# A decoder trunk's first stage: weights in halves of the contraction, half of the tokens later, tables on ScalarE's queue

## The chip, the core and the metric

The kernel runs on one NeuronCore of a Trainium2 chip. It is one launch. The metric is the device time of that launch in microseconds (us). Five engines work side by side, each with its own in-order queue: TensorE (PE, matrix products and transposes; PEld is its load of the stationary operand), VectorE (DVE), ScalarE (ACT), GpSimd (POOL) and SyncE (SP). Transfers from memory are asked for on SP's or ACT's queue ("SPq", "ACTq" in the profile) and run on 16 DMA engines.

## What is computed

Two decoder layers over 512 tokens of 1024 channels, in float32. The part that the change touches is the very beginning, the first even mixer's input projection:

```python
def even_mixer(x, w_in, conv_w, pool_w, pool_scale, w_out):
    p = x @ w_in                                   # 512 x 1024 by 1024 x 2048
    y_a = short_gated_conv(p[..., :3 * D_A], conv_w)
    y_b = multiscale_pool(p[..., 3 * D_A:], pool_w, pool_scale)
    return jnp.concatenate([y_a, y_b], axis=-1) @ w_out

for layer in range(DEPTH):                         # DEPTH = 2: even_mixer, then odd_mixer
    x = layer_norm(ALPHA * x + mix, ...)
    x = layer_norm(ALPHA * x + swiglu(x, ...), ...)
```

`odd_mixer` (forgetting attention beside a 31-tap convolution) and the two `swiglu` blocks follow. The parameter tables of both mixers' convolutions (`ev_conv_w`, `ev_pool_scale`, `od_dw_w`, `od_dw_b`, `od_cn_g`, `od_cn_b`) and the 4 x 128 x 128 matrix `ev_pool_w` are small inputs beside the weights.

## The kernel before

**Numbers.** Each float32 operand is split into a rounded part and a rest (`split`, L84 to L87: ACT copies the rounded part, `hi`; DVE or POOL subtracts it from the source, `lo`). A product is three matmuls that add into one PSUM bank: hi x hi, hi x lo, lo x hi (`mm3`, L89 to L92). So every weight costs one transfer, one ACT copy and one DVE or POOL subtraction before PE can use it.

**Tokens.** The 512 tokens are four tiles of 128 (`x0` to `x3`, 512 KB each). PE transposes each tile in eight 128 x 128 blocks (`transpose_x`, L128 to L150), and `split` makes `xh` and `xl` of them, channels on partitions. All later products stream `xh` and `xl`.

**The first block.** The last 512 columns of `w_in` feed the pooling mixer in four groups of 128 columns. Groups 0 and 1 come first: `START = "x0 x1 w0G x2 x3 w1G"` asks on SP's queue for two token tiles, the first weight block (all 1024 rows of 128 columns, `w0`), the other token tiles and the second weight block (`w1`). "G" says that POOL makes the `lo` part. `project(pus, ws, HALF)` then forms group 0 and group 1 for tokens 0 to 255 and for tokens 256 to 511: 2 x 2 x 8 x 3 = 96 matmuls with 256 columns, into two PSUM banks, `pus`. Six matmuls of the identity with itself (`WARM`, L125) run ahead of the first transpose.

**Tables.** `params()` asks on ACT's queue for six row tables (38 rows of 512 in all, `rows`), transposes them on PE (L575) and copies them to `par`. `pool_params()` loads `ev_pool_w` on SP's queue and splits it. `ln_params()` loads six rows of 8 x 128 on SP's queue and transposes them (L190).

**Order.** The framework's scheduler sets the order on all engines of this stage from a timeline that it estimates; inside `tc.manual_schedule` blocks the engines named there keep the order in which the code is written. Later stages (both SwiGLU blocks, PE in the attention) are in such blocks already. Each engine, and each of the two issuing queues, takes its instructions strictly in order. A transfer reports on one of eight counters, `DMAHW0` to `DMAHW7`, which are given out in turn; a transfer that is given a counter whose last transfer has not landed waits, at its place in the issuing engine's queue, until it has.

Of the kernel before, what the change touches and what calls it, by code (L numbers as in the profile page):

```python
# [10 lines left out]
F32 = mybir.dt.float32  # L11
F32R = mybir.dt.float32r
# [5 lines left out]
P = 128  # L18
# [6 lines left out]
DH = 512  # L25
# [10 lines left out]

CP = 900
WARM = 6
START = "x0 x1 w0G x2 x3 w1G"
SPLIT = [(0, 256), (256, 512)]  # L40
FIRST = 2
PLAIN = 4
# [18 lines left out]
def trunk(ctx, tc, x, ev_w_in, ev_conv_w, ev_pool_w, ev_pool_scale, ev_w_out, od_w_in,  # L61
          od_forget_b, od_dw_w, od_dw_b, od_cn_g, od_cn_b, od_w_out,
          ln_mix_g, ln_mix_b, ln_ffn_g, ln_ffn_b, ffn_w_in, ffn_w_out, out):
    nc = tc.nc
# [3 lines left out]
    rawp = pool("raw", 3)  # L68
    wtp = pool("wt", 8)
# [9 lines left out]
    def tpsum():  # L79
        return psum("tp")  # L80
# [3 lines left out]
    def split(hi, lo, src, eng=None):  # L84

        nc.scalar.activation(hi, src, AF.Copy)  # L86
        (eng or nc.vector).tensor_tensor(lo, src, f32(hi), op=ALU.subtract)  # L87
# [17 lines left out]
    def load_cols(w, c0, **kw):  # L105
        return load_split(w[:, c0:c0 + P].rearrange("(k p) c -> p k c", p=P), [KD, P], **kw)
# [8 lines left out]
    xs = [res.tile([P, D], F32, tag=f"x{t}", name=f"x{t}") for t in range(NT)]  # L115
    xh = res.tile([P, KD, S], F32R, tag="xh", name="xh")
    xl = res.tile([P, KD, S], F32R, tag="xl", name="xl")
# [10 lines left out]
    def transpose_x(t, gbt=None, tags=("tp", "tp")):  # L128

        for half in range(2):  # L130
            tp = psum(tags[half])
            for j in range(4):
                k = half * 4 + j
                nc.tensor.transpose(tp[:, j * P:(j + 1) * P], xs[t][:, k * P:(k + 1) * P], ident)
            src = tp
            if gbt is not None:
                src = wk.tile([P, S], F32, tag="sg", name="xt")
                for j in range(4):
                    k = half * 4 + j
                    blk = slice(j * P, (j + 1) * P)  # L140
                    if j < XA:
                        nc.scalar.activation(src[:, blk], tp[:, blk], AF.Identity,
                                             scale=gbt[:, 0, k:k + 1], bias=gbt[:, 1, k:k + 1])
                    else:
                        nc.vector.tensor_scalar(src[:, blk], tp[:, blk], gbt[:, 0, k:k + 1], gbt[:, 1, k:k + 1],
                                                op0=ALU.mult, op1=ALU.add)
            dst = (slice(None), slice(half * 4, half * 4 + 4), slice(t * P, (t + 1) * P))
            split(xh[dst], xl[dst], src.rearrange("p (j q) -> p j q", q=P))

    def project(accs, ws, ranges):  # L150

        for a, b in ranges:
            for acc, (wh, wl) in zip(accs, ws):
                for k in range(KD):
                    mm3(acc[:, a:b], wh[:, k, :], wl[:, k, :], xh[:, k, a:b], xl[:, k, a:b],
                        k == 0, k == KD - 1)

    ALL = [(0, S)]
# [405 lines left out]
    def params():  # L564

        rows = wk.tile([38, DH], F32, tag="sg", name="rows")
        nc.scalar.dma_start(rows[0:3, :], ev_conv_w[0])
        nc.scalar.dma_start(rows[3:4, :], ev_pool_scale)
        nc.scalar.dma_start(rows[4:35, :], od_dw_w[0])
        nc.scalar.dma_start(rows[35:36, :], od_dw_b)  # L570
        nc.scalar.dma_start(rows[36:37, :], od_cn_g)
        nc.scalar.dma_start(rows[37:38, :], od_cn_b)
        tp = tpsum()
        for j in range(4):
            nc.tensor.transpose(tp[:, j * 38:(j + 1) * 38], rows[:, j * P:(j + 1) * P], ident[:38, :38])  # L575
        nc.vector.tensor_copy(par, tp[:, :152].rearrange("p (j r) -> p j r", r=38))

    def even_mixer():
        w_in = ev_w_in[0]
# [4 lines left out]
        with tc.tile_pool(name="even", bufs=1) as ep:  # L584
# [3 lines left out]

            def pool_params():
                pwr = rawp.tile([P, 4, P], F32, tag="raw", name="pwr")  # L590
                nc.sync.dma_start(pwr, ev_pool_w[0].rearrange("g c d -> c g d"))
                pwh = ep.tile([P, 4, P], F32R, tag="pwh", name="pwh")
                pwl = ep.tile([P, 4, P], F32R, tag="pwl", name="pwl")
                split(pwh, pwl, pwr)
                return pwh, pwl
# [28 lines left out]
                                               op0=ALU.mult, op1=ALU.subtract)  # L624

            ws = []
            for item in START.split():
                i = int(item[1])
                if item[0] == "x":
                    nc.sync.dma_start(xs[i], x[0, i * P:(i + 1) * P, :])  # L630
                    transpose_x(i, tags=(("tp", "tp"), ("sc", "sc"), ("py", "cv"), ("tp", "tp"))[i])
                else:
                    ws.append(load_cols(w_in, 3 * DH + i * P, eng=nc.gpsimd if item[2] == "G" else None))
            pus = [psum("fl"), psum("fl")]
            project(pus, ws, HALF)
            pw = pool_params()
            params()
            ln_params()
            z = [pool_in(pus[g], g) for g in range(2)]
            for g in range(2, 4):  # L640
                w = load_cols(w_in, 3 * DH + g * P)
                pu = psum()
                project([pu], [w], ALL)
                z.append(pool_in(pu, g))
                pool_out(g - 2, *z[g - 2])
            for j in range(4):
# [454 lines left out]
```

## Time and profile before

| | |
|---|---|
| device time, 3 runs | median 1083.24 us (1083.21 to 1085.02) |
| the profiled execution, its own time | 1084.19 us |
| its span, first to last instruction | 1082.5 us |
| mean granted TensorE clock | 0.987 of full speed |
| PE busy | 1046.3 us, 97% |
| DVE, ACT, POOL busy | 744.3, 482.6, 179.5 us |
| DMA | 108.49 MB, mean 100 GB/s |

In timelines a row gives the start in us from the span's start, the duration, the engine, the line, the operation, out<-in and the count; in brackets stand the engine's idle time before the row and what ended it. In the tables by windows each engine has its busy time and, in brackets, its instructions; then come the granted clock of PE, the share of the 16 DMA engines that was busy, and the GB/s moved. A matmul's row is longer than its share of PE's time, since matmuls overlap: the step from one start to the next is what one costs in a row of many.

### The profile page before, as it was taken

Reading aid. Unit: us, or ns where it says so; the run is one execution under the profiler, and the core shown is the slowest. Engines: PE = TensorE matmul, PEld = TensorE weight load, DVE = VectorE, ACT = ScalarE, POOL = GpSimd, SP = SyncE. Lnnn points to the kernel's source line nnn. Section 1 sums busy time; section 2 is a strip of 40 time slices with the busy share of each in tenths; the row PEclk is TensorE's granted clock in tenths of the full one; section 3 lists DMA queues with packets and bytes.
Section 4 is the critical chain, followed back from the end, with each engine's and each line's share of the span. In section 5 each row is a group of like instructions: output and inputs, shape, how many; then the busy total and the mean of one; then the engine's idle time right before and its main releaser. Section 6 shows DMA issues by size and latency. Waiting matters only on the chain.

```text
span 1082.5 us, 16331 instructions
## 1 busy us (share of the span) xinstructions
PE 1046.3 (97%) x6631; PEld 938.1 (87%) x6631; DVE 744.3 (69%) x1027; ACT 482.6 (45%) x711; POOL 179.5 (17%) x163
## 2 busy tenths in 40 slices
PE   7999999999799999999999899999999799999997
PEld 7888889899688999988979777889899688999986
DVE  3845466888562788756479988466888562788746
ACT  4432233545321455443466889533545321455520
POOL 2000300000000000012499983610000000000003
PEclk8999999999899999999999999999999899999999
DMA  6433501631332431360233332311531333440522
GB/s 205 120 98 104 168 1 45 189 99 41 116 117 92 143 121 37 120 191 21 58 101 98 95 104 59 118 39 43 190 99 41 117 115 101 134 130 28 163 71 78
DMA packets 113482, 108.49 MB, mean 100 GB/s; under 512 B 5257, under 2 KB 94905, under 8 KB 113407
## 3 DMA queue, kind: packets, MB, share of 16 engines
q1 hardware_dynamic: 112784, 107.11, 32.2%
q8 instruction: 52, 0.85, 0.3%
q10 hardware_dynamic: 622, 0.34, 0.1%
q14 instruction: 24, 0.19, 0.1%
HBM read 103.17 MB, written 2.10 MB: 97 GB/s over the span
## 4 chain that ended last, share of the span: by engine, by line
PE 81%; DVE 8%; ACT 4%; issue 3%; DMA 2%; POOL 1%; SPq 0%; POOLq 0%; ACTq 0%; DVEq 0%
PE fl L388 14%; PE fl L91 9%; PE fl L92 9%; PE fl L90 9%; PE sc L388 7%; PE sc L91 5%; PE sc L92 5%; PE sc L90 5%; DVE sw L380 3%; PE py L91 2%; PE py L90 2%; PE py L92 2%; DVE sum L369 2%; PE cv L388 2%; PE cv L92 2%
## 5 line engine op out<-in xcount | busy, mean ns | idle before, releaser
L86 ACT ACTIVATE w<-raw 128x1024 fp32r<-128x1024 f32 x104 | 109.0, 1057 | 207.8 <-PE sc L91 77.9
L388 PE MATMUL fl<-T,sw 128*128 128x256 f32 x1296 | 160.5, 279 | 4.3 <-DVE sw L380 1.5
L388 PEld LDWEIGHTS fl<-T,sw 128*128 128x128 f32 x1296 | 153.9, 188 | 6.9 <-ACT u L396 2.5
L87 DVE TENSOR_TENSOR w<-raw,w 128x1024 fp32r<-128x1024 f32 x76 | 92.4, 1223 | 92.1 <-ACT w L86 91.7
L87 POOL TENSOR_TENSOR w<-raw,w 128x1024 fp32r<-128x1024 f32 x28 | 67.3, 2413 | 424.3 <-ACT w L86 410.7
L376 ACT ACTIVATE sw<-sum 128x1024 fp32r<-128x1024 f32 x72 | 76.0, 1060 | 104.6 <-DVE sum L369 73.5
L380 DVE TENSOR_TENSOR sw<-sum,sw 128x1024 fp32r<-128x1024 f32 x72 | 88.0, 1222 | 26.2 <-ACT sw L376 26.2
L388 PE MATMUL sc<-xh,sw 128*128 128x256 f32 x576 | 105.5, 278 | 0.0
L388 PEld LDWEIGHTS sc<-xh,sw 128*128 128x128 f32 x576 | 89.9, 188 | 0.1
L380 DVE TENSOR_TENSOR sw<-q,sw 128x1024 fp32r<-128x1024 f32 x54 | 65.4, 1221 | 29.2 <-ACT sw L376 29.1
L168 POOL TENSOR_TENSOR rs<-rs,neghalf 128x1 f32<-128x1 f32 x20 | 13.6, 681 | 402.2 <-DVE rs L167 396.2
L388 PE MATMUL sc<-xl,sw 128*128 128x256 f32 x288 | 80.1, 278 | 0.0
L90 PE MATMUL fl<-w,hh 128*128 128x512 f32 (+1 forms) x176 | 69.7, 396 | 8.8 <-ACT w L86 8.8
L376 ACT ACTIVATE sw<-q 128x1024 fp32r<-128x1024 f32 x54 | 56.3, 1050 | 45.3 <-DMA q<-in_ffn_w_in 45.3
L91 PE MATMUL fl<-w,hh 128*128 128x512 f32 (+1 forms) x176 | 69.6, 395 | 1.6 <-DVE w L87 1.6
L92 PE MATMUL fl<-w,hl 128*128 128x512 f32 (+1 forms) x176 | 69.3, 394 | 0.0
L704 DVE SCALAR_TENSOR_TENSOR cv<-hp,par,cv 128x512 f32<-128x512 f32 x84 | 63.1, 751 | 5.8 <-ACT cv L692 4.5
L369 DVE TENSOR_TENSOR sum<-q,q 128x1024 f32<-128x1024 f32 x36 | 43.9, 1219 | 25.7 <-DMA q<-in_ffn_w_in 25.7
L388 PE MATMUL fl<-xh,sw 128*128 128x256 f32 x288 | 53.8, 281 | 1.6 <-DVE sw L380 1.6
L91 PE MATMUL sc<-xl,w 128*128 128x256 f32 (+1 forms) x168 | 55.0, 329 | 0.0
L90 PE MATMUL sc<-xh,w 128*128 128x256 f32 (+1 forms) x168 | 54.9, 331 | 0.0
L92 PE MATMUL sc<-xh,w 128*128 128x256 f32 (+1 forms) x168 | 54.8, 328 | 0.0
(413 smaller groups left out, 2666.1 us busy)
## 6 DMA issues: line engine op xcount, KB each, us to landing
q<-in_ffn_w_in SPq DMA_DIRECT2D x72, 512.0 KB
raw<-in_ffn_w_out SPq DMA_DIRECT2D x44, 512.0 KB
raw<-in_od_w_in SPq DMA_DIRECT2D x20, 512.0 KB
raw<-in_ev_w_in SPq DMA_DIRECT2D x16, 512.0 KB
raw<-in_ffn_w_in SPq DMA_DIRECT2D x16, 512.0 KB
raw<-in_ev_w_out SPq DMA_DIRECT2D x8, 512.0 KB
raw<-in_od_w_out SPq DMA_DIRECT2D x8, 512.0 KB
x<-in_x SPq DMA_DIRECT2D x4, 512.0 KB
```

The source lines that it names most:

```text
L86: nc.scalar.activation(hi, src, AF.Copy)
L87: (eng or nc.vector).tensor_tensor(lo, src, f32(hi), op=ALU.subtract)
L90: nc.tensor.matmul(acc, lh, rh, start=start, stop=False)
L91: nc.tensor.matmul(acc, lh, rl, start=False, stop=False)
L92: nc.tensor.matmul(acc, ll, rh, start=False, stop=stop)
L168: nc.gpsimd.tensor_tensor(rs[:, 1:2], rs[:, 0:1], neghalf, op=ALU.pow)
L369: nc.vector.tensor_tensor(raw[name], raw[a], raw[b], op=ALU.add)
L376: nc.scalar.activation(g["A"][name][0], g["raw"][self.LEFT[name]], AF.Copy)
L380: nc.vector.tensor_tensor(lo, g["raw"][self.LEFT[name]], f32(hi), op=ALU.subtract)
L388: nc.tensor.matmul(acc, l[:, k, cols], r[:, k, :], start=start and i == k == m == 0, stop=stop and i == 1 and k == 3 and m == 2, skip_grou ...
L704: V.scalar_tensor_tensor(acc if i == KCONV - 1 else part, hp[:, i:i + S], tap(i), part, op0=ALU.mult, op1=ALU.add)
```

## The change

In the first block only:

- **First weights in halves of k.** Instead of two blocks of 1024 rows by 128 columns, two of 512 rows by 256 columns are loaded: `w0` holds rows 0 to 511 for groups 0 and 1, `w1` rows 512 to 1023. The same bytes are loaded, and the same 96 matmuls run, in four parts of 24: `A0` (first half of k, tokens 0 to 255), `A1` (second half of k), `B0`, `B1` (tokens 256 to 511). Within a part all hi x hi products come first, then hi x lo, then lo x hi.
- **Queues.** SP's queue asks for `x0`, `x1`, `w0`; ACT's queue asks, behind its first copies, for `w1` ("d1"), `x2`, `x3` ("d2", "d3"), the six tables ("pp") and, later, `ev_pool_w`.
- **Fill.** Twelve further matmuls of the identity with itself ("ww") stand behind the transposes of `x1`.
- **Order by hand.** PE, ACT and DVE keep the written order through the first block, `ev_pool_w`'s split and the split of the weights of groups 2 and 3. The tables' transposes come behind it. `w0`'s lo part moves from POOL to DVE; `w1`'s stays on POOL.

```diff
-START = "x0 x1 w0G x2 x3 w1G"
+KEEP = 12
+FIRSTS = "x0 d1 x1 d2 d3 pp w0 ww A0 w1 x2 A1 x3 B0 B1"
...
             def pool_params():
                 pwr = rawp.tile([P, 4, P], F32, tag="raw", name="pwr")
-                nc.sync.dma_start(pwr, ev_pool_w[0].rearrange("g c d -> c g d"))
+                nc.scalar.dma_start(pwr, ev_pool_w[0].rearrange("g c d -> c g d"))
...
-            for item in START.split():
-                i = int(item[1])
-                if item[0] == "x":
-                    nc.sync.dma_start(xs[i], x[0, i * P:(i + 1) * P, :])
-                    transpose_x(i, tags=(("tp", "tp"), ("sc", "sc"), ("py", "cv"), ("tp", "tp"))[i])
-                else:
-                    ws.append(load_cols(w_in, 3 * DH + i * P, eng=nc.gpsimd if item[2] == "G" else None))
             pus = [psum("fl"), psum("fl")]
-            project(pus, ws, HALF)
-            pw = pool_params()
-            params()
+            def first_block(i, a, b):
+                wh, wl = ws[i]
+                for m, (w, xt) in enumerate(((wh, xh), (wh, xl), (wl, xh))):
+                    for g, acc in enumerate(pus):
+                        for k in range(4):
+                            nc.tensor.matmul(acc[:, a:b], w[:, k, g * P:(g + 1) * P], xt[:, 4 * i + k, a:b],
+                                             start=i == m == k == 0, stop=i == 1 and m == 2 and k == 3)
+            raws = [rawp.tile([P, 4, 2 * P], F32, tag="raw", name="raw") for _ in range(2)]
...
+            load_x(0, nc.sync)
+            load_x(1, nc.sync)
+            load_w(0, nc.sync)
+            later = {1: lambda: load_w(1, nc.scalar), 2: lambda: load_x(2, nc.scalar),
+                     3: lambda: load_x(3, nc.scalar)}
+            with tc.manual_schedule(engines={mybir.EngineType.PE, mybir.EngineType.Activation,
+                                             mybir.EngineType.DVE}):
+                for item in FIRSTS.split():
+                    if item == "ww":
+                        for _ in range(KEEP):
+                            nc.tensor.matmul(warmup[:, :P], ident, ident, start=True, stop=True)
+                        continue
+                    if item == "pp":
+                        params_transposed = params()
+                        continue
+                    i = int(item[1])
+                    if item[0] == "x":
+                        transpose_x(i, tags=(("tp", "tp"), ("sc", "sc"), ("py", "cv"), ("tp", "tp"))[i])
+                    elif item[0] == "d":
+                        later[i]()
+                    elif item[0] == "w":
+                        ws.append([wtp.tile([P, 4, 2 * P], F32R, tag="wt", name="w") for _ in range(2)])
+                        split(*ws[i], raws[i], nc.gpsimd if i else None)
+                    else:
+                        first_block(i, *HALF["AB".index(item[0])])
+                pw = pool_params()
+                wn = [load_cols(w_in, 3 * DH + g * P) for g in (2, 3)]
+            params_transposed()
```

ACT's queue at the start of the program, before the change. `xh_78` are copies of transposed tokens out of PSUM, `w_145` the hi part of `w0` out of `raw_143`, `rows_289` the six tables; the waits are on counters of engines and transfers.

```order
L567 DMA rows_289<-in_ev_conv_w 3x512
L123 ACT_TABLE_LOAD
L123 ACTIVATE warm_85<-warm_85 128x1 [waits DVE_49]
L568 DMA rows_289<-in_ev_pool_scale 1x512
L569 DMA rows_289<-in_od_dw_w 31x512
L570 DMA rows_289<-in_od_dw_b 1x512
L571 DMA rows_289<-in_od_cn_g 1x512 [waits DMAHW1_49]
L86 ACTIVATE xh_78<-tp_114 128x4x128 [waits PE_49]
L572 DMA rows_289<-in_od_cn_b 1x512 [waits DMAHW3_49]
L86 ACTIVATE xh_78<-tp_121 128x4x128 [waits PE_49]
L86 ACTIVATE xh_78<-sc_129 128x4x128 [waits PE_49]
L86 ACTIVATE w_145<-raw_143 128x1024 [waits DMAHW4_49]
```

All six tables are asked for ahead of the second token copy, and `w0`'s copy comes behind three token copies. The same queue now, from the copies of `x1` (`sc`) to the copies of the two weight halves (`raw_115` is `w0`, `raw_116` is `w1`):

```order
L87 ACTIVATE xh_78<-sc_137 128x4x128 [waits PE_49]
L87 ACTIVATE xh_78<-sc_144 128x4x128 [waits PE_49]
L646 DMA x2_76<-in_x 128x1024
L646 DMA x3_77<-in_x 128x1024
L575 DMA rows_153<-in_ev_conv_w 3x512
L576 DMA rows_153<-in_ev_pool_scale 1x512 [waits DMAHW1_49]
L577 DMA rows_153<-in_od_dw_w 31x512 [waits DMAHW3_49]
L578 DMA rows_153<-in_od_dw_b 1x512 [waits DMAHW5_49]
L579 DMA rows_153<-in_od_cn_g 1x512 [waits DMAHW7_49]
L580 DMA rows_153<-in_od_cn_b 1x512 [waits DMAHW1_49]
L87 ACTIVATE w_160<-raw_115 128x1024 [waits DMAHW2_49]
L87 ACTIVATE w_200<-raw_116 128x1024
```

The tables now stand between the token copies and the weight copies. In this program the counters go to the transfers in this order: `x0` 0, `x1` 1, `w0` 2, `w1` 3, `x2` 4, `x3` 5, `ev_conv_w` 6, the first row of `ln_params` 7; `ev_pool_scale` gets 1 again, `od_dw_w` 3, `od_dw_b` 5, `od_cn_g` 7 and `od_cn_b` 1 for a third time.

PE's queue before, from the identity matmuls (L126) over the token transposes (L134) to the first products (L90 to L92):

```order
L126 MATMUL cv<-ident 128x128 x6
L134 MATMUL tp<-ident,x_74 128x128 x8
L134 MATMUL sc<-ident,x_75 128x128 x8
L134 MATMUL py<-ident,x_76 128x128 x4
L134 MATMUL cv<-ident,x_76 128x128 x4
L90 MATMUL fl<-xh,w 128x256
L91 MATMUL fl<-xl,w 128x256
L134 MATMUL tp<-ident,x_77 128x128 x8
L92 MATMUL fl<-xh,w 128x256
```

And now (L664 are the twelve fill matmuls, L640 the products; `x_74` to `x_77` are the token tiles):

```order
L135 MATMUL sc<-ident,x_75 128x128 x8
L664 MATMUL cv<-ident 128x128 x12
L640 MATMUL fl<-xh,w 128x256 x8
L640 MATMUL fl<-xl,w 128x256 x8
L640 MATMUL fl<-xh,w 128x256 x8
L135 MATMUL py<-ident,x_76 128x128 x4
L135 MATMUL cv<-ident,x_76 128x128 x4
L640 MATMUL fl<-xh,w 128x256 x8
L640 MATMUL fl<-xl,w 128x256 x8
L640 MATMUL fl<-xh,w 128x256 x8
L135 MATMUL tp<-ident,x_77 128x128 x8
```

The transposes of `x2`, which PE took as soon as `x1` was done, now stand behind part `A0`, and those of `x3` behind `A1`. In the odd layer's attention the estimated timeline has also swapped some neighbours on ACT, DVE and POOL; PE's order there is the same.

More of the change, by code (lines that the diff above doesn't have):

```diff
@@ L566, in params, with transposed @@
         rows = wk.tile([38, DH], F32, tag="sg", name="rows")
+        def transposed():
+            tp = tpsum()
+            for j in range(4):
+                nc.tensor.transpose(tp[:, j * 38:(j + 1) * 38], rows[:, j * P:(j + 1) * P], ident[:38, :38])
+            nc.vector.tensor_copy(par, tp[:, :152].rearrange("p (j r) -> p j r", r=38))
         nc.scalar.dma_start(rows[0:3, :], ev_conv_w[0])
@@ L572, in params @@
         nc.scalar.dma_start(rows[37:38, :], od_cn_b)
[L573 to L576, printed above, removed]
+        return transposed
     def even_mixer():
@@ new lines, in even_mixer, with load_x, load_w @@
+            raws = [rawp.tile([P, 4, 2 * P], F32, tag="raw", name="raw") for _ in range(2)]
+            def load_x(i, eng):
+                eng.dma_start(xs[i], x[0, i * P:(i + 1) * P, :])
+            def load_w(i, eng):
+                eng.dma_start(raws[i], w_in[i * DH:(i + 1) * DH, 3 * DH:3 * DH + 2 * P].rearrange(
+                    "(k p) c -> p k c", p=P))
+            load_x(0, nc.sync)
[3 more added lines that the diff above has]
+                     3: lambda: load_x(3, nc.scalar)}
@@ L640, in even_mixer @@
             for g in range(2, 4):
-                w = load_cols(w_in, 3 * DH + g * P)
                 pu = psum()
-                project([pu], [w], ALL)
+                project([pu], [wn[g - 2]], ALL)
                 z.append(pool_in(pu, g))
```

## The prediction, on record before the result

> **What bounds the kernel now.** I read three views in this order: PE's waits, the first microseconds on PE and ACT in order of time, and the same stretch by windows. From the start to 210 us PE waits for others like this:
>
> ```profile
> PE py L134 <- DMA x<-in_x: 4.6, 1, 4.6
> PE cv L126 <- POOL sum L606: 1.6, 1, 1.6
> PE fl L388 <- DVE sw L380: 1.0, 2, 0.8
> PE fl L388 <- ACT sw L376: 0.7, 1, 0.7
> PE tp L134 <- DMA x<-in_x: 0.2, 1, 0.2
> ```
>
> Between the wait for a token tile (`py` holds the transposes of `x2`) and the first Strassen products (L388, in the SwiGLU) PE has none. So whatever PE gains or loses in the first block it keeps one for one: the stages behind it are tied to PE's progress, and no transfer there is asked for at a fixed time. The question is when PE finishes the 96 products of the first block. The stretch on PE and ACT:
>
> ```profile
> 1.56 2.93 PE L126 MATMUL cv<-ident 128*128 128x128 f32 x12 [1.56 <-POOL sum L606]
> 4.67 1.63 PE L134 MATMUL tp<-ident,x 128*128 128x128 f32 x8 [0.18 <-DMA x<-in_x]
> 6.14 1.04 PE L134 MATMUL sc<-ident,x 128*128 128x128 f32 x8
> 6.34 0.60 ACT L86 ACTIVATE xh<-tp 128x512 fp32r<-128x512 f32 x1
> 10.40 1.06 ACT L86 ACTIVATE w<-raw 128x1024 fp32r<-128x1024 f32 x1 [2.97 <-DMA raw<-in_ev_w_in]
> 11.54 2.36 POOL L87 TENSOR_TENSOR w<-raw,w 128x1024 fp32r<-128x1024 f32 x1 [9.81 <-ACT w L86]
> 11.82 1.11 PE L134 MATMUL py<-ident,x 128*128 128x128 f32 x4 [4.64 <-DMA x<-in_x]
> 13.44 0.56 PE L90 MATMUL fl<-xh,w 128*128 128x256 f32 x1
> 26.91 0.28 PE L91 MATMUL fl<-xl,w 128*128 128x256 f32 x1
> 27.03 0.28 PE L92 MATMUL fl<-xh,w 128*128 128x256 f32 x1
> 27.24 0.44 PE L575 MATMUL tp<-ident,rows 38*128 38x38 f32 x4
> 27.68 0.50 PE L90 MATMUL fl<-xh,w 128*128 128x512 f32 x1
> ```
>
> PE stops at 7.18, goes on at 11.82 with `x2`, and from there runs without a gap to 27.24, where the tables' transposes follow the last product: 15.42 us for 16 transposes and 96 products. A product in the row costs the step between starts, 0.12 us. Part of the 15.42 is spent at half clock:
>
> ```profile
> 5.82:9.24 3.42, 1.36 (x12) 1.12 (x10) 1.88 (x3) 1.60 (x3) 0.00 (x0) 1.00 1.07 355
> 9.24:12.65 3.41, 0.83 (x4) 0.83 (x5) 0.67 (x1) 1.54 (x2) 1.11 (x1) 0.50 0.95 278
> 12.65:16.06 3.41, 3.41 (x18) 3.41 (x17) 1.72 (x4) 1.89 (x4) 1.25 (x1) 0.50 0.09 23
> 16.06:19.48 3.42, 3.42 (x31) 3.42 (x30) 2.49 (x3) 2.25 (x4) 1.90 (x1) 1.00 0.54 153
> ```
>
> The columns are PE, PEld, DVE, ACT, POOL, then clock, DMA share and GB/s. The clock falls to 0.50 at 9.24, while PE is idle, and comes back at 16.06. PE works 4.24 us at half speed and loses 2.12 us by it.
>
> **What the change takes away.** The first weights come late because of the tables. At 13 to 16 us DMA is 9% busy, and still SP waits for `x3` and `w1` (it can issue behind them only at 13.16 and 14.82):
>
> ```profile
> 1.71 0.30 ACTq L569 DMA_DIRECT2D rows<-in_od_dw_w  x1
> 2.04 0.34 ACTq L570 DMA_DIRECT2D rows<-in_od_dw_b  x1
> 4.65 0.23 ACTq L571 DMA_DIRECT2D rows<-in_od_cn_g  x1
> 5.98 0.38 SPq L97 DMA_DIRECT2D raw<-in_ev_w_in  x1
> 13.16 0.27 SPq L188 DMA_DIRECT2D rows<-in_ln_ffn_b  x1
> 14.82 0.27 SPq L188 DMA_DIRECT2D rows<-in_ln_mix_b  x1
> rows<-in_od_dw_w ACTq DMA_DIRECT2D x1, 62.0 KB
> ```
>
> About one engine in sixteen is late with its share, and a table of 62 KB was asked for just ahead of `w0`. The Trainium skill, "DMA: Bandwidth & Descriptors", section "Why a DMA increments its semaphore by 16 and not by 1", says that a transfer is spread over the largest number of engines up to 16 that divides its slowest dimension; 31 rows would all go to one engine, which agrees with this tail. With the tables behind `x3`, `w0` should land where the rate puts it: `x1` has landed at 5.98 (SP's next issue waited for it), plus 512 KB at 355 GB/s, 1.48 us, gives 7.4 instead of 10.4. That is the change's possible gain.
>
> **What it adds.** The queue order of ACT has the tables between the copies of `x1` and the copy of `w0`, and three of their issues wait at that place for a transfer to land: `od_dw_w` for `w1`, `od_dw_b` for `x3`, `od_cn_b` for `ev_pool_scale`. That such a wait holds ACT is in the rows above: `od_cn_g` was free to go at 2.38 and went at 4.65, when `x0` had landed and PE began its transposes at 4.67. So `w0`'s copy, `w1`'s copy and the copies of `x2` and `x3` all stand behind the landing of `x3`, and every product of part `A0` behind `w0`'s copy. PE's transposes of `x2`, which filled the wait before, stand behind `A0`.
>
> When does `x3` land? ACT can ask for `w1` with the second copy of `x0`, at about 6.4, and for `x2` and `x3` with the second copy of `x1`, whose transposes end at 7.18: about 7.3 and 7.7 (two issues took 0.86 us on SP):
>
> ```profile
> 0.80 0.86 SPq L630 DMA_DIRECT2D x<-in_x  x2
> 185.81 3.60 DMA q<-in_ffn_w_in
> ```
>
> The second row, from the chain of waits, is a block of 512 KB with nothing ahead of it: 3.60 us from issue to landing. So `w1` lands at 10.0, `x2` and `x3` 1.48 us behind each other, `x3` at 12.9. Bounds: alone it would land at 7.7 + 3.6 = 11.3; at most as late as before, about 13.1. I take 12.9, since the rate of 355 GB/s is held over the whole stretch before. The Trainium skill, the same page, section "Issuing engines are not separate DMA queues", says that a second issuing queue saves issue time only; by it too the three blocks share one rate and the sum stands.
>
> Then three more issues (0.34 + 0.23 + 0.23), so `w0`'s copy starts at 13.7 and ends at 14.76; with 0.09 of passing on, as from 11.46 to POOL's start at 11.54 before, PE starts `A0` at 14.85.
>
> **The sum.**
> - PE resumes at 14.85 instead of 11.82: +3.03 us.
> - The work from there is the same, 16 transposes and 96 products. PE has been idle from the end of the fill to 14.85. The fill costs twelve times what a warm-up matmul costs at full clock: six took 2.93 at half, so twelve take 2.93, and they end at 10.1. That is 4.74 us of idle against 4.64 before, so the half-clock loss is the same: 0. The fill is hidden by the wait. If the wait were gone, it would hold `A0` until 10.1.
> - `lo` of `w0` (now on DVE) and of `w1` (POOL, 2.36 us behind a copy that ends at about 15.8) are ready before their products: the first to need one stands 16 products of twice 0.12 behind 14.85, at 18.7. 0.
> - `B0` follows `x3`'s transposes at once and needs the first copy (0.60) of them, of which half is covered by the second four transposes: +0.25.
> - Behind the block, after the tables' transposes (0.44, from 27.24 to 27.68) come the products of groups 2 and 3. They need their weight copies, which stand on ACT behind `ev_pool_w`. That is asked for at about 24.7, with the second copy of `x3`; 256 KB take between 2.9 (3.60 less half of 1.48) and 3.6 us. The copies of it and of two weights, about 0.6 + 2 x 1.06, then end between 30.3 and 31.0, against a need at 30.5 + 0.44 = 30.95: 0, with a cover of 0.7 at most.
> - Fewer rows on SP, DVE instead of POOL for `w0`: beside PE's work, 0.
>
> In all +3.3 us. Against the profiled execution's own 1084.19 (span 1082.5) that is 1087.5; this execution is 0.95 above the median of the runs shown, 1083.24, so on the median's footing the forecast is **1086.5 us**, 0.3% slower.
>
> **Rivals.**
>
> *A: `x3` lands early and the clock holds.* At the bound 11.3, `w0`'s copy ends at 13.16 and PE starts at 13.25, 3.15 us behind the fill. If the clock stays up, the end moves by 13.25 - 11.82 - 2.12 + 0.25 = -0.4 us; if it drops for one window of 3.41 us, by +1.3: about 1084, no change. By the Trainium skill, "TensorE: Matmul & The Clock Gate", Part 1, the clock is judged over free-running windows of some 3.4 us and drops after an idle one, so that a gap of 4.74 would often not contain a whole idle window, and then even the forecast's start would cost only +1.2 us, 1084.4. The trace has the windows (9.24 and 16.06 are two of them apart), but not that mildness:
>
> ```profile
> 596.32:599.74 3.42, 1.02 (x4) 0.86 (x5) 3.25 (x6) 3.28 (x8) 3.42 (x4) 1.00 0.02 5
> 599.74:603.15 3.41, 3.41 (x13) 2.58 (x12) 3.37 (x8) 2.16 (x5) 3.33 (x4) 0.50 0.43 108
> ```
>
> Here a window with PE 30% busy was enough for the drop. A gap of 4.74 us takes at least 2.37 us out of some window, a third busy at most. So A needs the early landing.
>
> *B: the copies are not held (faster).* If ACT reached `w0` at its landing, 7.4, and behind the token copies at 8.0, `w0` would be copied by 9.1, PE would go from the fill at 10.1 straight into `A0` at full clock, and the block would last 15.42 - 2.12 + 0.25 = 13.55 us, to 23.7: -3.6 us, 1079.6. It decides itself by whether ACT's copy starts before about 9. For it speaks the early landing of `w0`; against it the waits in ACT's order.
>
> *C: the held-back work comes due (slower still).* `ev_pool_w` late by the 3.6 bound and copies of the sums out of the two banks behind it (both groups now end together, where group 0's bank was free at 25.77) leave DVE with `pwl`, two weights' `lo` and both groups' window sums at once. DVE was busy 16.4 of 20 us between 40 and 60, so a backlog of 3 to 4 us is absorbed late, and PE could stand 1 to 3 us more: 1088.5.
>
> ```profile
> 20.00:40.00 20.00, 20.00 (x120) 17.71 (x120) 13.90 (x22) 8.21 (x12) 0.39 (x5) 1.00 0.60 163
> 40.00:60.00 20.00, 20.00 (x89) 16.54 (x89) 16.44 (x26) 7.51 (x11) 0.52 (x5) 1.00 0.36 102
> 25.77 0.58 ACT L602 ACTIVATE u<-fl 128x512 f32<-128x512 f32 x1
> ```
>
> **How the numbers follow.** Forecast 0.60, A 0.17, B 0.08, C 0.15. I call no change what lies within 0.2% (2.2 us, about what can be told apart here). The forecast's own range is +1.8 to +4.6 us (landing of `x3` from 11.4 to 13.1, the phase of the clock's windows, and swaps in the attention, which I put at 1 us either way), a tenth of it within the bound. Slower: 0.54 + 0.15 = 0.69, rounded to 0.68; same 0.06 + 0.17, with a little more for a shifted phase, 0.24; faster 0.08. The range for 8 in 10 takes in most of A and C and leaves out B: 1082.5 to 1089.5.
>
> **What would show it.** Right: in the changed kernel's timeline ACT's issue of `od_dw_b` comes at 12 to 13 us, `w0`'s copy (L87, `w<-raw`) starts behind it at 13 to 14, PE has a gap of over 4 us behind L664 that is put down to ACT, the clock is 0.50 at the start of L640, and the tables' transposes (L572) start near 30.5. Wrong: `w0`'s copy starts before 10 us, or the clock stays at 1.00 through the first products, or the tables' transposes start before 27.2.

## The result and the profile after

The changed kernel takes 1091.23 us (median of 6 runs, 1088.12 to 1092.86); the kernel before, on the same chip, 1083.45 (6 runs, 1079.33 to 1086.11). The ratio is 1.0070, 95% interval 1.0048 to 1.0091: **slower by 0.7%**, some 7.8 us. The sign is the forecast's; the size is not: 1086.5 was forecast, with a range up to 1089.5. A second measurement of the same kernel gave 1.0080 (1.0059 to 1.0102). The profiled execution shown here took 1092.86 us (span 1091.1). Executions of one kernel differ by up to 10 us (28 of the kernel before on one chip took 1080.47 to 1090.02), so the times below are medians, with intervals of the ratio to the kernel before.

PE's waits from the start to 210 us, now:

```profile
PE fl L640 <- ACT w L87: 6.4, 1, 6.4
PE cv L127 <- POOL ident masks.py:199: 1.6, 1, 1.6
PE fl L389 <- DVE sw L381: 0.4, 1, 0.4
PE fl L640 <- ACT xh L87: 0.2, 1, 0.2
```

Where PE waited 4.6 us for a token tile it now waits 6.4 us for ACT's copy of `w0`. The same stretch on ACT and PE in order of time (rows of two answers of the timeline, ACT's first):

```profile
8.02 0.45 ACTq L646 DMA_DIRECT2D x<-in_x  x1
8.50 0.56 ACTq L575 DMA_DIRECT2D rows<-in_ev_conv_w  x1
9.11 0.23 ACTq L576 DMA_DIRECT2D rows<-in_ev_pool_scale  x1
10.01 0.23 ACTq L577 DMA_DIRECT2D rows<-in_od_dw_w  x1
14.69 0.23 ACTq L578 DMA_DIRECT2D rows<-in_od_dw_b  x1
15.26 0.26 ACTq L580 DMA_DIRECT2D rows<-in_od_cn_b  x1
15.57 2.00 ACT L87 ACTIVATE w<-raw 128x1024 fp32r<-128x1024 f32 x2 [7.29 <-DMA rows<-in_od_cn_g]
...
7.43 2.84 PE L664 MATMUL cv<-ident 128*128 128x128 f32 x24
16.68 2.08 PE L640 MATMUL fl<-xh,w 128*128 128x256 f32 x8 [6.41 <-ACT w L87]
26.38 1.21 PE L640 MATMUL fl<-xh,w 128*128 128x256 f32 x8 [0.25 <-ACT xh L87]
32.32 0.44 PE L572 MATMUL tp<-ident,rows 38*128 38x38 f32 x4
32.76 0.50 PE L91 MATMUL sc<-xh,w 128*128 128x512 f32 x1
```

This is the mechanism that was forecast, row by row. `od_dw_w` goes at 10.01, when `w1` has landed; then ACT stands for 4.45 us at `od_dw_b`, whose counter is that of `x3`, although `w0` landed at 7.17. `x3` lands at 14.67, and behind three more issues `w0`'s copy starts at 15.57. PE has had nothing to do since 10.27. The tables' transposes, which mark the end of the first block, come at 32.32 instead of 27.24: **5.08 us of the loss are there**. The clock over it (columns as in the prediction):

```profile
10.32:13.73 3.41, 0.00 (x0) 0.00 (x0) 0.00 (x0) 0.00 (x0) 0.00 (x0) 1.00 0.62 240
13.73:17.15 3.42, 0.47 (x2) 0.47 (x3) 0.49 (x1) 1.58 (x2) 0.00 (x0) 0.50 0.09 31
17.15:20.56 3.41, 3.41 (x18) 3.41 (x18) 0.74 (x1) 0.43 (x1) 2.46 (x1) 0.50 0.39 104
20.56:23.97 3.41, 3.41 (x31) 3.41 (x31) 1.29 (x2) 1.09 (x2) 0.00 (x0) 1.00 0.73 207
```

PE starts at half clock and stays there until 20.56, for 3.88 us of work, 1.94 lost.

The block's loss is carried on unchanged: the first Strassen product, the next landmark that all kernels share, comes 5.07 us later. Of the kernel before:

```profile
198.57 0.28 PE L388 MATMUL fl<-xh,sw 128*128 128x256 f32 x1
```

and of the changed one:

```profile
203.64 0.28 PE L389 MATMUL fl<-xh,sw 128*128 128x256 f32 x1
```

Behind that, more is lost. PE's waits from 430 us to 1060 us, the kernel before:

```profile
PE fl L90 <- ACT w L86: 4.6, 2, 4.2
```

and the changed one:

```profile
PE fl L91 <- ACT w L87: 8.2, 3, 4.2
```

In the changed kernel PE waits 3.6 us more for weight copies, at two places: 448.62 (2.62 us, and the clock is at 0.50 for two windows behind it) and 1021.63 (1.35 us), ahead of the first products of the late out-projection (the products with `ffn_w_out`) in each SwiGLU. The first of them, on ACT, on PE, and in the list of transfers:

```profile
450.13 1.06 ACT L87 ACTIVATE w<-raw 128x1024 fp32r<-128x1024 f32 x1 [2.13 <-DMA raw<-in_ffn_w_out]
451.24 0.79 PE L91 MATMUL fl<-w,hh 128*128 128x512 f32 x1 [2.62 <-ACT w L87]
q8 instruction: 1, 0.02, 0.7%
```

The weight block, asked for at 444.25, had landed on 15 engines at 448.01 and on the last at 450.11. The third row is not data: at 447.74 a block of 16 KB of instructions was fetched. On which of the 16 engines it ran the trace does not tell. No part of the prediction had such a thing.

### The profile page after: what moved, and what is told of

The parts are those of the page before. It is cut to its first block, busy times and chain, and to the rows that moved or that the text cites. A ratio compares the mean times of both kernels' runs of the same rounds, so it can differ in the third digit from the quotient of the medians.

```text
span 1091.1 us, 16381 instructions
## 1 busy us (share of the span) xinstructions
PE 1047.5 (96%) x6655; PEld 939.0 (86%) x6655; DVE 742.8 (68%) x1028; ACT 482.1 (44%) x711; POOL 177.4 (16%) x162
## 4 chain that ended last, share of the span: by engine, by line
PE 76%; DVE 13%; ACT 5%; issue 3%; DMA 2%; POOL 0%; ACTq 0%; POOLq 0%; DVEq 0%; SPq 0%
PE fl L389 11%; PE fl L92 8%; PE fl L91 8%; PE fl L93 8%; PE sc L389 6%; PE sc L91 5%; PE sc L92 5%; PE sc L93 5%; DVE sw L381 5%; DVE sum L370 2%; PE py L91 2%; PE py L92 2%; PE py L93 2%; ACT sw L377 2%; PE cv L91 2%
## 5 line engine op out<-in xcount | busy, mean ns | idle before, releaser
L92 PE MATMUL fl<-w,hh 128*128 128x512 f32 (+1 forms) x176 | 69.6, 396 | 1.4 <-DVE w L88 1.4
L92 PE MATMUL sc<-xl,w 128*128 128x256 f32 (+1 forms) x168 | 55.0, 329 | 0.0
```

The lines of the kernel that those rows point to most:

```text
L92: nc.tensor.matmul(acc, lh, rl, start=False, stop=False)
```

## Experiments

To compare starts, I read the first Strassen product in each profile: 198.57 and 198.84 us in two profiles of the kernel before (mean 198.7), 203.64, 203.80 and 204.12 in three of the changed one. "Start" below is that row less 198.7; for the changed kernel it is +4.9 to +5.4.

**My theory** of the loss at the start: ACT's queue is held by the table issue that waits for `x3`, `w0`'s copy stands behind it, and PE carries the loss. **Rivals:** the halves of k, the token tiles asked for on ACT, or the tables' transfers cost by themselves; and, for what is lost behind the start, chance.

**1. Tables behind the copies of `x3`.**

```diff
-FIRSTS = "x0 d1 x1 d2 d3 pp w0 ww A0 w1 x2 A1 x3 B0 B1"
+FIRSTS = "x0 d1 x1 d2 d3 w0 ww A0 w1 x2 A1 x3 pp B0 B1"
```

> The changed kernel with the six table issues and their waits moved behind ACT's copies of `x3`. My theory (the wait of a table's issue for `x3` holds ACT's queue, and with it `w0`'s copy): `w0`'s copy starts near 8.5 us instead of 15.57, PE goes from the fill (end 10.27) into the first products near 10.3 at full clock, the tables' transposes come near 24 us instead of 32.32, and the time falls by 8.6 us to about 1082.6, or to about 1080 if the 2.5 us that the changed kernel lost behind 400 us is not there. Rival (the held queue is not what costs; the blocks in halves of k, or the transfers asked for in ACT's stream, are late by themselves): first products not before 13 us, and the time at 1088 or more.

Measured: ratio 1.0049 (1.0029 to 1.0069), start +4.0. PE's and SP's rows:

```profile
10.37 1.19 PE L640 MATMUL fl<-xh,w 128*128 128x256 f32 x8
24.29 0.44 PE L572 MATMUL tp<-ident,rows 38*128 38x38 f32 x4
28.22 0.79 PE L91 MATMUL fl<-xh,w 128*128 128x512 f32 x1 [3.43 <-ACT w L87]
...
22.92 5.74 SPq L98 DMA_DIRECT2D raw<-in_ev_w_in  x3
```

The first block did as the theory says: products at 10.37, tables' transposes at 24.29, 8.0 us earlier. Then PE stood 3.43 us, and the clock fell to half for 6.83 us. The same trap had closed on another queue: SP's load of group 2's weights waits for the counter that `od_dw_w` holds, and `od_dw_w`, asked for at 18.95 and moved by one DMA engine, lands at 22.84. So the held queue is shown twice; of the 8.6 us expected at the start about 1.2 came, since the wait only moved.

**2. The tables one item later, behind `w0`'s copy.**

```diff
-FIRSTS = "x0 d1 x1 d2 d3 pp w0 ww A0 w1 x2 A1 x3 B0 B1"
+FIRSTS = "x0 d1 x1 d2 d3 w0 pp ww A0 w1 x2 A1 x3 B0 B1"
```

> The changed kernel with the six table issues moved by one item only, from ahead of `w0`'s copy to between `w0`'s and `w1`'s copy on ACT. Theory (ACT stands at `od_dw_b` until `x3` has landed, whatever is behind it): `w0` is copied at 8.9 to 9.9 us, `A0` runs from 10.4 to 13.4 and the transposes of `x2` to 14.5, then PE waits for `w1`'s copy, which starts at 15.3 to 15.6, and goes on at 16.4 to 16.8; the tables' transposes come at 26.5 to 28.5 us (the later, if the clock falls in that gap), 4 to 6 us earlier than in the changed kernel, the time falls to 1085 to 1087. Rival (the hold is not what PE keeps one for one): less than 2 us of it, 1089 or more.

Measured: 1.0048 (1.0030 to 1.0067), start -0.8, and +0.9 in a second profile.

```profile
13.79 0.23 ACTq L578 DMA_DIRECT2D rows<-in_od_dw_b  x1
14.68 1.06 ACT L87 ACTIVATE w<-raw 128x1024 fp32r<-128x1024 f32 x1 [5.85 <-DMA rows<-in_od_cn_g]
...
15.79 1.21 PE L640 MATMUL fl<-xh,w 128*128 128x256 f32 x8 [2.17 <-ACT w L87]
26.56 0.44 PE L572 MATMUL tp<-ident,rows 38*128 38x38 f32 x4
```

ACT again stands until `x3` has landed (13.77), whatever is behind; now it is `w1`'s copy. The start is 4 to 6 us better than the changed kernel's, as expected. The time is 5 us over before although the start is even: the largest loss behind the start in the study. One part of it is not the tables' doing: the estimated timeline has swapped other neighbours in the attention here, and the stretch from PE's row `sc<-qk` behind the wait of 3.1 us for `aug` to its first row `cv<-ident,npair` takes 76.42 and 74.88 us in the two profiles, against 73.04 and 73.09 in the kernel before.

> The changed kernel with the tables between `w0`'s and `w1`'s copy once more, for its profile: its median lay 5.2 us over before, its profiled execution 4.5 us below that median. Theory 1: the start as in its first profile (tables' transposes near 26.6 us), and a gap at an awaited weight block behind 400 us. Theory 2: the start itself varies (the clock falls in the gap ahead of `w1`'s copy in some executions, and the transposes come near 28.5).

That second profile has its transposes at 28.23 (the clock was at half for one window) and a gap of 1.73 us at 444.93, ahead of the late out-projection's products: both theories hold a part.

**3. Tables on SP's queue.** All six issues, as the first here:

```diff
-        nc.scalar.dma_start(rows[0:3, :], ev_conv_w[0])
+        nc.sync.dma_start(rows[0:3, :], ev_conv_w[0])
```

> The changed kernel with the six tables asked for on SP behind `w0`, not on ACT: nothing but copies and three large issues is left in ACT's queue at the start. Theory (it is the waiting issue in ACT's queue that costs, not the tables' transfers): `w0`'s copy starts at 8 to 9 us and the first products near 10.3; the one engine with 31 rows may make `x2` and `x3` up to 2.4 us late, so the tables' transposes come between 24 and 26.5 us, and the time is 1080 to 1085. Rival (the tables' transfers themselves cost): first products behind 13 us, time at 1088 or more.

Measured: 1.0010 (0.9996 to 1.0024), start -1.0; tables' transposes at 26.37, at the late end of what was expected.

```profile
7.26 0.45 ACTq L649 DMA_DIRECT2D raw<-in_ev_w_in  x1
10.45 0.84 ACTq L646 DMA_DIRECT2D x<-in_x  x2
11.34 2.01 ACT L87 ACTIVATE w<-raw 128x1024 fp32r<-128x1024 f32 x2 [2.49 <-DMA rows<-in_od_cn_b]
```

The tables' transfers do not cost 5 us. But my statement that ACT was now free was wrong: the counters are handed on in turn, so that now the issues of `w1`, `x2` and `x3` on ACT got counters of `w0` and of tables, and ACT stood until `od_dw_b` had landed (10.43). First products at 12.45, not 10.3.

**4. Tables first, as before.**

```diff
-FIRSTS = "x0 d1 x1 d2 d3 pp w0 ww A0 w1 x2 A1 x3 B0 B1"
+FIRSTS = "pp x0 d1 x1 d2 d3 w0 ww A0 w1 x2 A1 x3 B0 B1"
```

> The changed kernel with the one step undone that the prediction blames: the six table issues stand first in ACT's order again, ahead of the copies of `x0`, as in the kernel before; weights in halves of k, ACT's issues of `w1`, `x2` and `x3`, and the fill stay. Theory (the place of the tables is the whole loss): `w0` has its one late engine again (about 10.4 us), `w1` is asked for when `od_dw_w` has landed (about 9.2), the first products come near 11.6 us, the tables' transposes near 24.5 us, that is 2.7 us earlier than in the kernel before and 7.8 earlier than in the changed one; the time is 1079 to 1081. Rival (halves of k, or the token tiles asked for on ACT, cost by themselves): the tables' transposes at 27.2 us or later, time at 1082 or more.

Measured: 1.0003 (0.9981 to 1.0024), start +0.3. This undoes one step of the change and takes back all of its loss. It does not turn it into the gain that I expected, and both signs of the rival came (transposes not before 27.2, time over 1082). The rows show another hold in place of the old one:

```profile
9.62 0.41 ACTq L649 DMA_DIRECT2D raw<-in_ev_w_in  x1
11.11 1.06 ACT L87 ACTIVATE w<-raw 128x1024 fp32r<-128x1024 f32 x1
...
12.22 1.44 PE L640 MATMUL fl<-xh,w 128*128 128x256 f32 x8 [2.25 <-ACT w L87]
27.66 0.44 PE L572 MATMUL tp<-ident,rows 38*128 38x38 f32 x4
```

ACT stands at `w1`'s issue for `od_dw_w` (landed 9.60), with the copies of `x1` behind it, and `w0`'s last engine is at 10.34 again. That halves of k and token tiles on ACT cost by themselves is answered by experiment 1: with both, and no hold, the block ended 3 us earlier than in the kernel before.

**5. The one late engine.** The kernel before, with `od_dw_w` in two issues:

```diff
-        nc.scalar.dma_start(rows[4:35, :], od_dw_w[0])
+        nc.scalar.dma_start(rows[4:20, :], od_dw_w[0, :16])
+        nc.scalar.dma_start(rows[20:35, :], od_dw_w[0, 16:])
```

> The kernel before with `od_dw_w`'s 31 rows loaded by two issues, of 16 and 15 rows, instead of one. Theory (31 rows go to one of 16 engines, which is then 2.4 us late with its share of everything behind it, `w0` first): `w0` has landed on every engine near 8.0 us instead of 10.38, PE goes on with `x2` near 9.5 instead of 11.82, the tables' transposes come near 26 us instead of 27.24 (2.3 us earlier, of which more work at half clock takes back 1.2), the time about 1.1 us less, 1082.3. Rival (the late engine is late for another reason): `w0` at 10.4 us as before, and the same time.

Measured: **0.9965 (0.9952 to 0.9978), faster**, start -3.5. (The scheduler put the tables' transposes into the block here, so they are no landmark.)

```profile
8.77 1.06 ACT L86 ACTIVATE w<-raw 128x1024 fp32r<-128x1024 f32 x1 [2.04 <-DMA raw<-in_ev_w_in]
...
10.08 0.66 PE L134 MATMUL py<-ident,x 128*128 128x128 f32 x4 [2.63 <-DMA x<-in_x]
...
5.18:8.60 3.42, 1.95 (x16) 1.47 (x14) 1.29 (x2) 1.09 (x2) 0.00 (x0) 1.00 1.04 324
8.60:12.01 3.41, 1.72 (x14) 1.55 (x15) 1.67 (x3) 3.09 (x5) 2.10 (x1) 1.00 1.08 346
```

`w0` is copied 1.6 us earlier and PE goes on 1.74 earlier. The larger part came unasked: PE was idle for 2.63 us only, the windows were 57% and 50% busy, and the clock stayed at 1.00, where I had put 1.2 us of extra loss. In the landing records, 31 rows report from one engine and 16 rows from 16. The rule of the Trainium skill that the prediction named ("DMA: Bandwidth & Descriptors", section "Why a DMA increments its semaphore by 16 and not by 1") gives just that for 31 and for 16 rows.

The same edit in the changed kernel, tables still ahead of `w0`'s copy:

> The changed kernel with `od_dw_w` in 16 and 15 rows, the tables still ahead of `w0`'s copy. Its order on ACT, DVE and POOL in the attention is that of the kernel before. Theory (the table of 31 rows, in flight beside `x2` and `x3`, is what makes three to six engines late with them): `x3` has landed at 13.0 to 13.8 us instead of 14.7, the first products come at 15.2 to 15.9, the tables' transposes at 31.0 to 31.6; and theory on the rest (the changed order in the attention costs the gap of 1.19 us that three profiles with it show near 630 us, and six without it do not): no such gap, so that the time is 1087.5 to 1089.5. Rival (`x3` is late for another reason, and the attention's order costs nothing): transposes at 32.4, time 1091.

Measured: 1.0079 (1.0058 to 1.0099), tables' transposes at 32.32, 33.10 and 32.54 in three profiles, start +5.0 to +5.7. `x3` landed at 13.88, but behind one more issue, and at 14.14 and 14.82 in the next two, against 14.67, 14.70 and 14.23 in the changed kernel. So here the split buys nothing, and that the 31-row table makes `x3` late is not borne out.

> The changed kernel with the split table once more, for its profile alone: its median lay 8.9 us over before, while its one profiled execution was 5.5 us below that median. Theory 1 (a weight block of `ffn_w_out` or `ffn_w_in` lands late on one engine, with PE waiting, and the clock falls behind it, as at 448 us in the changed kernel): a gap of PE of 1 to 3 us behind 400 us that the first profile of this kernel lacks, with a late last engine at a DMA of weights. Theory 2 (PE's rows themselves are spaced wider somewhere, as between 227 and 260 us in the kernel before): a drift without a gap. The start as before: first products at 16.3 within 0.4 us.

> The same kernel a third time, for the same question: under theory 1 a new gap at a place with awaited weights (near 448, 840 or 1015 us), under theory 2 a drift of 1 to 3 us without one.

Their times were 1094.09 and 1090.49 us. Both have a gap ahead of the second SwiGLU's late out-projection that the kernel before lacks (1.97 us at 1022.21, 1.78 us at 1017.28), each with one late engine: theory 1. The former also falls back by 2.8 us between 200 and 300 us against the second profile of before, without such a gap: theory 2 has a part as well.

**6. The fill.** One number, here the largest; 0, 8 and 16 likewise. PE's order is otherwise the same, and that on ACT, DVE, POOL and SP is the same word for word.

```diff
-KEEP = 12
+KEEP = 38
```

> The changed kernel with 38 fill matmuls instead of 12: at 0.237 us each they end near 16.4 us, just ahead of the first product (16.68). Theory (the idle wait drops the clock, and PE worked 3.88 us at half speed behind it): clock 1.00 throughout, the tables' transposes at 30.4 instead of 32.32, the time 1.9 us less, 1089.3. Rival (the clock costs nothing, since the stages behind set the end): the same time, 1091.2.

> The changed kernel without its 12 fill matmuls. Theory (the fill is hidden by the wait for ACT and does not hold the clock): PE is idle from about 7.4 instead of 10.3, the first products come at 16.7 as in the changed kernel, the clock is at 0.50 when they start and comes back near 20.6, the tables' transposes come at 32.4 within 0.5 us, the time is 1091.3 within 1 us. Rival (the 12 keep part of the clock, or hold PE): transposes over 1 us later, or earlier.

> The changed kernel with 8 fill matmuls instead of 12. In 17 profiles so far, PE waits for a late weight copy near 445 and 1016 us only where a block of PE's instructions is fetched between 0.9 and 2.6 us behind the issue of the first `ffn_w_out` block of that stage; in the changed kernel the fetch comes 2.5 to 3.5 and 0.9 to 3.3 us behind it, without the fill 6.6 and 8.2, in the kernel before 6.6 to 7.1 and 8.6 to 9.7. Theory (the place of the fetch, which hangs on the number of PE's instructions ahead of it, costs 1.5 to 3 us of the rest): with 4 matmuls less the fetch comes near +3.9 and +4.1, neither block is late, neither gap comes, and the time is 1088 to 1089.8 at the start of the changed kernel (tables' transposes at 32.3 to 33.7). Rival (the fetch is chance or of no effect): the gaps are there again in one of the two places, the time 1091.3.

> The changed kernel with 16 fill matmuls, hidden by the wait as the 12 are. Theory of the fetch: it comes 4 matmuls' instructions earlier, near +1.6 to +2.4 and -0.3 to +1 us from the block's issue; the first block is late by 1 to 2 us on one engine and PE has a gap of 1.4 to 2.6 near 449 us, the second place has one only if the fetch is behind the issue; time 1089.5 to 1092. Rival: no more gaps than with 8.

| fill matmuls | first product | tables' transposes | start | ratio to before |
|---|---|---|---|---|
| 0 | 17.08 | 33.65 | +6.3 | 1.0050 (1.0034 to 1.0066) |
| 8 | 16.69 | 32.43 | +5.1 | 1.0051 (1.0032 to 1.0069) |
| 12 (the change) | 16.68, 16.71, 16.26 | 32.32, 32.48, 32.80 | +4.9 to +5.4 | 1.0070, 1.0080 |
| 16 | 16.98 | 32.55 | +5.2 | 1.0037 (1.0021 to 1.0052) |
| 38 | 16.05 | 29.98 | +2.6 | 1.0037 (1.0024 to 1.0050) |

With 38, PE is idle for 0.98 us and the clock holds, as expected: 2.3 to 2.8 us at the start. Without fill the clock falls earlier (9.36) and comes back at 23.02: the start is 1.2 us worse than I expected from a hidden fill. And yet 0, 8 and 16 have a shorter median than 12, by 2 to 5 us, at the same or a worse start. The intervals of 0 and 8 overlap with both of 12's (1.0048 to 1.0091 and 1.0059 to 1.0102); that of 16 lies clear of the second and touches the first. So what is lost behind the start seems to hang on something as inert as the number of PE's instructions ahead of it. Of the kernel with 8, the place where the changed kernel waited 2.62 us:

```profile
448.83 0.50 PE L91 MATMUL fl<-w,hh 128*128 128x512 f32 x1 [0.38 <-ACT w L87]
```

I then read, in the 19 profiles of the study, when the nearest block of instructions is fetched against the issue of the first `ffn_w_out` block at the two places (38 cases), and whether the block's last engine lands more than 0.5 us behind its fifteenth. Fetched 0.24 to 2.48 us behind the issue: late in 13 of 13, by 0.5 to 1.5 us. 2.54 to 3.83 us behind: in 4 of 14, by 0.7 to 2.1 us. Further off: in 0 of 11. The wait of 2.62 us that led here is one of those 4: its fetch came 3.49 us behind the issue, so the bound of 2.6 us in the expectation for 8 was read wrongly. In the kernel before the fetch stands 6.6 to 9.7 us behind the issue, in both profiles and at both places; with 12 fill matmuls 0.9 to 3.5; without fill 6.6 and 8.2; with 8, 3.2 and 2.8; with 16, 0.2 and 0.5. A third profile of the changed kernel fits:

> The changed kernel a third time, for its profile: the start as in the two before (first products at 16.7, tables' transposes at 32.3 to 32.5), the gap of 1.19 us near 632 us again (it comes with this kernel's order in the attention), and behind the start 2 to 4 us more than in the kernel before, under theory 1 from one or two late weight blocks, under theory 2 without a gap.

It has late blocks at both places (gaps of 1.77 us at 450.18 and 1.43 us at 1018.96). So the change moved fetches close behind the issues of two awaited weight blocks, and in 4 of 6 cases one engine was late there; in the kernel before in 0 of 4. That the fetch makes it late is inferred from these counts. Their share of the time is not settled: from the first Strassen product to the end, the seven profiles without a late block take 880.1 to 885.7 us (mean 882.3), the twelve with one or two 880.0 to 888.0 (mean 884.0). With 16 both blocks are late, by 0.5 and 0.8 us, with gaps of 0.86 and 1.24, and the time is not 1089.5 or more as I expected but 1087.33; and the kernel of experiment 4 has both gaps (1.51 and 0.96) with a time that its start explains.

**7. A version that beats both.** SP asks for `x0`, `x1`, both weight halves, `x2`, `x3`, then for the tables; no table in one piece on one engine.

```diff
-KEEP = 12
-FIRSTS = "x0 d1 x1 d2 d3 pp w0 ww A0 w1 x2 A1 x3 B0 B1"
+KEEP = 6
+FIRSTS = "d1 d2 d3 pp x0 x1 w0 ww A0 w1 A1 x2 x3 B0 B1"
...
-            later = {1: lambda: load_w(1, nc.scalar), 2: lambda: load_x(2, nc.scalar),
-                     3: lambda: load_x(3, nc.scalar)}
+            later = {1: lambda: load_w(1, nc.sync), 2: lambda: load_x(2, nc.sync),
+                     3: lambda: load_x(3, nc.sync)}
...
-        nc.scalar.dma_start(rows[4:35, :], od_dw_w[0])
+        nc.sync.dma_start(rows[4:20, :], od_dw_w[0, :16])
+        nc.sync.dma_start(rows[20:35, :], od_dw_w[0, 16:])
```

The other five table issues go to `nc.sync` too.

> A kernel in which no waiting issue stands in ACT's queue and no table goes to a single engine ahead of the blocks: SP asks for `x0`, `x1`, both halves of the weights, `x2`, `x3` and then for the tables, with `od_dw_w` in 16 and 15 rows; both halves' products on the first 256 tokens come ahead of the transposes of `x2`; 6 fill matmuls. Theory (what costs are ACT's held queue and the one late engine): `w0` has landed at 7.2 us and is copied by 8.5, the first products come at 9.0 at full clock, the block ends near 22.8 us, 4.4 us earlier than in the kernel before, the time 4 to 5 us less than before: 1077 to 1078. Rival (the rows behind, not the first block, set what is gained: groups 2 and 3 wait for weights asked for behind the tables): a gap of over 2 us ahead of their products, and the time not below that of the kernel before with the split table, 1078.2.

Measured: **0.9966 (0.9951 to 0.9980), faster**, 1079.73 us, start -4.3.

```profile
8.73 1.21 PE L641 MATMUL fl<-xh,w 128*128 128x256 f32 x8 [0.43 <-ACT w L87]
22.80 0.44 PE L572 MATMUL tp<-ident,rows 38*128 38x38 f32 x4
23.46 0.50 PE L91 MATMUL sc<-xh,w 128*128 128x512 f32 x1 [0.15 <-ACT w L87]
```

The block ends at 22.80, as worked out, and there is no gap of 2 us behind it. The time of 1077 to 1078 did not come. The kernel before with the split table alone is as good (0.9965, start -3.5), so this run does not show that the halves of k and the new order of products gain anything beyond the split table, nor that they cost anything once nothing waits in ACT's queue.

**8. The kernel before once more.**

> The kernel before once more, unchanged, for its profile: how much of its start repeats. Theory: `w0` again has one late engine near 10.4 us, PE goes on near 11.8 and the tables' transposes come at 27.2 within 0.5 us; the 2.9 us that PE lost between 227 and 300 us in the first profile are partly missing, since five other profiles lack them. Rival: the first profile's start was itself an unlucky one, and the transposes come over 0.7 us earlier; the changed kernel's loss at the start is then larger than 5.1 us.

Its start repeats (tables' transposes at 27.52, `w0`'s last engine at 10.67, PE goes on at 12.12), and its time is 1081.91 (0.9990, 0.9978 to 1.0002). The 2.9 us between 227 and 300 us are partly missing, as expected: that much of one execution is chance.

> The changed kernel once more, unchanged, beside the kernel before on this chip. Theory 1 (the start costs 5.1 us and the attention, whose order on DVE, ACT and POOL differs from the kernel before in this kernel alone, costs 1 to 3 us more): the tables' transposes at 32 to 32.5 us again, and a time 6 to 8 us over before. Theory 2 (the part behind the first block is chance: where a block of instructions is fetched at the moment when a weight block is awaited): the gap of 2.62 us at 448.6 us is missing or elsewhere, and the time is 4.5 to 6 us over before.

The changed kernel's start repeats as well (32.48). No gap over 1 us at 448 or 1021 this time, with fetches 2.6 and 3.3 us behind the issue, and still 1.0080, where theory 2 had 4.5 to 6 us: this execution (1091.26 us) was as slow as the third profile's with its two late blocks (1090.27), so late blocks are not needed for the loss behind the start.

The attention has a part, as theory 1 says. The stretch named in experiment 2 takes 74.31, 74.30 and 74.32 us in the three profiles of the changed kernel, 73.04 and 73.09 in the two of before: 1.25 us. Seven profiles have the order of before (or all but the same) and at most one window at half clock there: 72.87 to 73.28. With the changed order it is 74.30 to 74.32 in six profiles, the fills of 8, 16 and 38 among them. A second window at half clock adds a like amount (74.37 to 74.67 in three profiles with the old order, 75.33 without fill). That is how the changed kernel with the split table, which keeps the old order, can lose as much there in two of its three profiles (74.48 and 74.67; 73.28 in the first).

## Why the prediction was wrong

Two steps failed. The landing of `x3` was put too early, which makes 1.8 us of the miss at the start, and what came behind the first block was put at nothing, which makes 2.7 to 3.6 us more.

- **What is held, and by what: right.** ACT stands at `od_dw_b` for `x3` (experiments 1, 2 and 4 move the hold or take it away). Rivals A and B are out: the landing was late, the clock fell, the copies were held. Of the signs, the gap (6.41) and the clock (0.50) came; `od_dw_b`, `w0`'s copy and the tables' transposes came 1.6 to 1.8 us behind the times named.
- **"So `w1` lands at 10.0, `x2` and `x3` 1.48 us behind each other, `x3` at 12.9": mis-sized.** `w1` did land at 9.98. `x3` landed at 14.67, outside the bounds of 11.3 and 13.1: it was asked for at 8.02, 0.3 us later than worked out, and in this profile 13 of its 16 engines were there at 13.09, the last three 1.6 us later. The spread of the engines was left out, and "at most as late as before" was no bound. From issue to landing `x3` took 6.65, 6.45 and 6.96 us in the changed kernel, 6.50 and 6.11 in experiment 2, 5.37 with the tables behind it in experiment 1 (one profile), against the 5.2 forecast. That the tables in flight delay it is likely, not shown; with the large one split it still took 5.68, 6.96 and 6.84.
- **The rest of the sum held.** From 14.67: three issues and the copy to 16.68 (2.01 against 1.95 forecast); the half-clock loss 1.94 against 2.12; the stall at `x3`'s copy 0.25 as forecast; fill ended at 10.27 (10.1); no wait ahead of groups 2 and 3, so rival C is out at its place. 16.68 less 11.82, less 0.18, plus 0.25 is 4.93; 5.08 was measured, 3.3 forecast.
- **"Whatever PE gains or loses in the first block it keeps one for one": right up to the Strassen products (5.07), wrong as an end of the account.** The time lost 7.8 to 8.7 us, 2.7 to 3.6 more than the start. The attention's swaps, for which 1 us either way stood in the range and nothing in the sum, cost 1.25. The sentence "no transfer there is asked for at a fixed time" overlooked transfers that stand in no queue of the program, the fetches of instructions: in two of three executions PE waited at weight blocks that landed late beside one. How much of the 2.7 to 3.6 us that is, and what the rest is, stays open.
- **"The fill is hidden by the wait": right for PE's start within 0.4 us, wrong for the time.** Four matmuls more or fewer, at the same start, went with medians 2 to 5 us lower; why is not shown.

## What to carry to other kernels

Before an issue is moved into an engine's queue, write down which counter it will get and what last used it: an issue waits in place, and everything behind it on that engine waits too, and adding or moving one transfer changes the counters of all later ones (experiments 1, 3 and 4 each moved the trap to another issue). Look at a late transfer by engines: a table of 31 rows ahead of the first weights cost 3.5 us at the start and 0.35% of the time, as much as all of experiment 7 gained, and two issues of 16 and 15 rows cured it. Where a few us count, compare several profiles of each kernel at shared landmarks, and vary something inert, such as the number of fill matmuls, before a late loss is put down to the edit's own logic.

## What the runs showed of the hardware

- The list of transfers has 52 fetches of 16 KB of instructions in each profile, of 875 to 2020 ns; from one to the next PE starts about 255 matmuls and weight loads. Fetched 0.24 to 2.48 us behind the issue of an awaited block of 512 KB, it came with one engine 0.5 to 1.5 us late, 13 times of 13.
- The clock has no clean threshold for its fall in these windows of 3.41 us: it fell behind one with PE 40% busy (the kernel before) and held behind two with 50% and 57% (experiment 5), but in experiment 7 it fell behind one with 57% (200.02 to 203.44). After a fall it came back only behind a window with PE busy 86% or more (2.94 us, without fill, from 292.67), and stayed at half behind one with 84% (2.88 us, the split table's third profile, from 600.62).
- `od_dw_w`, 62 KB in 31 rows, took 3.9 us on its one engine (18.95 to 22.84 in experiment 1), with small tables and, from 20.30, the 256 KB of `ev_pool_w` asked for beside it.
